# The opening of a one-layer decoder kernel rebuilt: smaller first groups, part of a vector-matrix product on TensorE, half the partial sums returned to PSUM

## The chip, the cores and the metric

The kernel runs on one core of one Trainium2 chip. The metric is the time of one execution on the device, in microseconds (us). The core has a matrix engine (TensorE, PE in the profile; its weight loads are PEld), a vector engine (VectorE, DVE), an activation engine (ScalarE, ACT), GpSimd (POOL) and SyncE (SP), which here only issues DMAs. Each engine runs its own list of instructions in order; the lists wait for each other through semaphores. TensorE adds its results up in PSUM, 8 banks of 128 x 512 f32.

## The reference, cut to what matters

One layer, 256 tokens, model width 2048, everything in float32. A conditioning vector c gives six modulation vectors; two of them (shift1, scale1) shape the normalised input h, and every projection of the layer reads h.

```python
mod = silu(c) @ w_ada + b_ada                  # (2048) @ (2048, 6*2048)
shift1, scale1, gate1, shift2, scale2, gate2 = split(mod, 6)
h = rms_norm(x, norm1_gain) * (1 + scale1) + shift1
proj = h @ w_in                                # (256, 2048) @ (2048, 13840)
# stick-breaking attention, dilated attention, gated linear attention on parts of proj,
# three sigmoid branch gates, an output projection
x = x + gate1 * mixing(h)
h = rms_norm(x, norm2_gain) * (1 + scale2) + shift2
x = x + gate2 * ((silu(h @ w_gate) * (h @ w_up)) @ w_ffn_out)
```

## The kernel before

**Products in three matmuls.** Each weight tile arrives by DMA as f32 (raw), ScalarE casts it to fp32r (whi, line 144), VectorE subtracts to get the remainder (wlo, line 145), and each product is three matmuls (lines 150 to 152): h-high by whi, h-high by wlo, h-low by whi. `load_weights` issues the DMAs on SP's queue, 512 KB (two chunks of 128 rows by 512 columns) at a time, with four buffers each of raw, whi and wlo. `block` runs such a product over a range of 128-row chunks k and both 128-token tiles t, into two PSUM banks.

**The opening.** h needs shift1 and scale1, that is 16.8 MB of w_ada, before its first product. So the 16 chunks of h are made in four groups, `GROUPS = ((0, 3), (3, 7), (7, 11), (11, 16))`. For a group, `ada_group` loads w_ada's columns for these chunks, row chunk by row chunk. VectorE multiplies each piece by the matching column of silu(c) and adds it to an accumulator `ada` (`ada_mac`, lines 245 and 247). At the end one-column matmuls against a column of ones (`column_sum`, line 290) sum the accumulator over its partitions, `finish_columns` (lines 296 and 299) adds the bias and folds in the gain, and `make_h` (lines 370 to 372) writes h's high and low parts for one chunk. A group of five is done in two pieces. While the 13 column blocks A[0..12] of the projection (512 columns each) run over the chunks of group g, `ada_group` for group g+1 is fed in between them, at lower urgency than the weights.

**Partial sums.** The first group's results are copied from PSUM to A[b] by ScalarE (line 400); each later group's are added to A[b] by VectorE (line 402). `orders` turns the order of the blocks round from group to group, and the last block of a group stays in its PSUM banks and is continued by the next group (`carry`). The accumulators of the blocks have four PSUM banks (`psa`), everything else four more (`psm`). In the last group the blocks are mixed with the attention parts, and further projections (r and the gates) that read all of h follow.

**The start.** c comes first, then silu(c). `XAT = 4` pieces of the first group's w_ada are issued ahead of x; then `norm1` squares x on ScalarE (line 349), gets 1/rms (`rsqrt`), scales x on ScalarE (line 356), turns it with 32 PE transposes (line 360) and copies it to xT (line 361). `load_vectors` brings gains and biases: three DMAs on SP's queue, seven on GpSimd's, into scratch tiles shared with norm1, then two transposes.

**Who sets the order.** The program is written as a data flow; a scheduler at build time orders each engine's list by priorities. `prio` raises one, `tc.issue_after` keeps instructions of one engine behind a given one, and `tc.keep_in_program_order` pins one.

Of the kernel before, what the change touches and what calls it, by code (L numbers as in the profile page):

```python
# [10 lines left out]
F32 = mybir.dt.float32  # L11
# [23 lines left out]
XAT = 4  # L35
AHEAD = 4000
FIN = 13
GROUPS = ((0, 3), (3, 7), (7, 11), (11, 16))
# [27 lines left out]
def trunk(ctx: ExitStack, tc: tile.TileContext, I, out):  # L66
# [55 lines left out]
    def load_weights(src, k0, k1, c0, w=NB, spare=()):  # L122
# [6 lines left out]
        with prio():  # L129
# [19 lines left out]
    def mm3(ps, lh, ll, rh, rl, start, stop):  # L149
        nc.tensor.matmul(ps, lh, rh, start=start, stop=False)  # L150
        nc.tensor.matmul(ps, lh, rl, start=False, stop=False)  # L151
        state["mm"] = nc.tensor.matmul(ps, ll, rh, start=False, stop=stop)  # L152

    def block(pss, act, src, k0, k1, c0, base=0, w=None, tiles=range(NT), go_on=False, more=False):
# [3 lines left out]
        for k in range(k0, k1):  # L158
# [6 lines left out]
            for t in tiles:  # L165
                h, l = act(base + k, t)
                mm3(pss[t], h, l, wh, wl, k == k0 and not go_on, k == k1 - 1 and not more)
# [11 lines left out]
    nc.scalar.copy(ones_r, ones)  # L179
# [7 lines left out]
    crow = scr([P, P])  # L187
# [11 lines left out]
    rows = scr([P, P])  # L199
    brow = scr([P, P])  # L200
# [3 lines left out]
    def load_vectors():  # L204
        nc.sync.dma_start(rows[16:32, :], by_chunk("norm1_gain"))
        nc.sync.dma_start(brow[0:96, :], by_chunk("b_ada"))
        nc.sync.dma_start(rows[32:48, :], by_chunk("norm2_gain"))
        for r, name in (
            (ROW_SBQ, "sb_q_gain"),
            (ROW_SBK, "sb_k_gain"),  # L210
            (ROW_DILQ, "dil_q_gain"),
            (ROW_DILK, "dil_k_gain"),
        ):
            nc.gpsimd.dma_start(rows[r : r + 1, :], I[name])
        nc.gpsimd.dma_start(rows[ROW_GB : ROW_GB + 4, :], by_chunk("b_gla_a"))
        nc.gpsimd.dma_start(rows[ROW_GG : ROW_GG + 2, :], by_chunk("gla_out_gain"))
        nc.gpsimd.dma_start(rows[0:16, :], by_chunk("c"))
# [116 lines left out]
    def norm1():  # L334
        xin = [S(f"A{9 + j}", [P, 2, NB]) for j in range(4)]
        for t in range(NT):
            for hf in range(2):
# [3 lines left out]
                )  # L341
        for t in range(NT):
            ss2 = small([P, 2])
            for hf in range(2):
                junk = scr([P, 512])
                xs = xin[2 * t + hf]
                pa = small([P, 2])
                for q in range(2):
                    nc.scalar.activation(junk, xs[:, q, :], AF.Square, accum_out=pa[:, q : q + 1])
                nc.vector.tensor_add(ss2[:, hf : hf + 1], pa[:, 0:1], pa[:, 1:2])  # L350
            ss = small([P, 1])
            nc.vector.tensor_add(ss, ss2[:, 0:1], ss2[:, 1:2])
            rstd = rsqrt(ss, 1.0 / D, [P, 1])
            for hf in range(2):
                xs = xin[2 * t + hf]
                nc.scalar.activation(xs, xs, AF.Copy, scale=rstd)
                for q in range(2):
                    ps = misc_bank([P, 4, P])
                    for i in range(4):
                        nc.tensor.transpose(ps[:, i, :], xs[:, q, i * P : (i + 1) * P], ident)  # L360
                    nc.scalar.copy(xT[2 * hf + q][:, :, t * P : (t + 1) * P], ps)
# [20 lines left out]
    up, down = list(range(13)), list(range(12, -1, -1))  # L382
    orders = (up[1:] + up[:1], up, down)
    carried = []

    def proj_block(g, b, w=None, carry=False):
        k0, k1 = GROUPS[g]
        go_on = bool(carried)
        pss = carried.pop() if go_on else [acc_bank() for _ in range(NT)]
        block(pss, h_at, w_in, k0, k1, b * NB, w=w, go_on=go_on, more=carry)  # L390
# [667 lines left out]
```

## Time and profile before

| | |
|---|---|
| median of 3 runs | 1647.3 us (1646.39 to 1650.2) |
| profiled execution, its own time | 1653.2 us |
| span of the profile (first to last instruction) | 1651.4 us |
| PE, DVE, ACT busy in the span | 1605.1, 1136.2, 773.0 us |
| first projection matmul | 36.88 us |
| mean granted TensorE clock | 0.993 |

The profile is one execution; its span and the 1.8 us around it make its own time. Busy times of different engines overlap and don't add up to the span. A matmul's row ends when its result is out of the pipeline, so matmuls that follow each other overlap in the records; the distance from start to start is what counts. "Granted clock" is the share of full TensorE speed.

### The profile page before, as it was taken

Reading aid. Unit: us, or ns where it says so; the run is one execution under the profiler, and the core shown is the slowest. Engines: PE = TensorE matmul, PEld = TensorE weight load, DVE = VectorE, ACT = ScalarE, POOL = GpSimd, SP = SyncE. Lnnn points to the kernel's source line nnn. Section 1 sums busy time; section 2 is a strip of 40 time slices with the busy share of each in tenths; the row PEclk is TensorE's granted clock in tenths of the full one; section 3 lists DMA queues with packets and bytes.
Section 4 is the critical chain, followed back from the end, with each engine's and each line's share of the span. In section 5 each row is a group of like instructions: output and inputs, shape, how many; then the busy total and the mean of one; then the engine's idle time right before and its main releaser. Section 6 shows DMA issues by size and latency. Waiting matters only on the chain.

```text
span 1651.4 us, 19878 instructions
## 1 busy us (share of the span) xinstructions
PE 1605.1 (97%) x7293; PEld 1324.2 (80%) x7293; DVE 1136.2 (69%) x1367; ACT 773.0 (47%) x1073; POOL 6.0 (0%) x14
## 2 busy tenths in 40 slices
PE   3999999999999999899998999999999999999998
PEld 3788888888878887688887788888888888888887
DVE  5789997787888476866987556766755555554453
ACT  5554446556755444344444644444444444433332
POOL 1000000000000000000000000000000000000000
PEclk8999999999999999999999999999999999999999
DMA  8899986445698778987997467877666566565663
GB/s 299 311 320 323 330 286 217 140 140 166 219 314 296 230 230 309 310 276 263 324 313 268 151 229 258 269 255 258 234 191 190 181 190 192 190 202 194 206 207 111
DMA packets 194561, 395.91 MB, mean 240 GB/s; under 512 B 12898, under 2 KB 27912, under 8 KB 194464
## 3 DMA queue, kind: packets, MB, share of 16 engines
q1 hardware_dynamic: 194240, 394.63, 71.9%
q8 instruction: 57, 0.93, 0.2%
q14 instruction: 40, 0.33, 0.1%
q0 software_dynamic: 224, 0.01, 0.0%
HBM read 392.50 MB, written 2.10 MB: 239 GB/s over the span
## 4 chain that ended last, share of the span: by engine, by line
PE 82%; DMA 7%; DVE 6%; issue 2%; ACT 2%; SPq 1%; DVEq 0%; ACTq 0%
PE acc L150 26%; PE acc L151 26%; PE acc L152 26%; DVE wlo L145 2%; DVE T L247 2%; DMA raw<-w_in 2%; DMA raw<-w_out 2%; ACT whi L144 1%; PE misc L592 1%; PE misc L290 1%; PE misc L846 1%; DVE ada L247 1%; DMA A<-x 1%; DMA raw<-w_br_gla 0%; DMA OS<-w_ada 0%
## 5 line engine op out<-in xcount | busy, mean ns | idle before, releaser
L145 DVE TENSOR_TENSOR wlo<-raw,whi 128x1024 fp32r<-128x1024 f32 (+1 forms) x548 | 653.3, 1197 | 422.2 <-ACT whi L144 420.1
L144 ACT CAST whi<-raw 128x1024 fp32r<-128x1024 f32 (+1 forms) x548 | 563.8, 1032 | 734.2 <-PE acc L152 555.4
L151 PE MATMUL acc<-wlo,H 128*128 128x512 f32 x1576 | 617.7, 392 | 1.7 <-DVE wlo L145 1.7
L150 PE MATMUL acc<-whi,H 128*128 128x512 f32 x1576 | 616.4, 392 | 2.5 <-ACT whi L144 2.5
L152 PE MATMUL acc<-whi,H 128*128 128x512 f32 x1576 | 616.8, 392 | 0.0
L151 PEld LDWEIGHTS acc<-wlo,H 128*128 128x128 f32 x1576 | 297.0, 189 | 64.3 <-DVE wlo L145 4.0
L150 PEld LDWEIGHTS acc<-whi,H 128*128 128x128 f32 x1576 | 296.8, 188 | 64.4 <-ACT whi L144 3.4
L152 PEld LDWEIGHTS acc<-whi,H 128*128 128x128 f32 x1576 | 296.8, 188 | 62.7 <-DVE H L372 0.9
L150 PE MATMUL acc<-whi,A 128*128 128x512 f32 x312 | 123.1, 396 | 2.7 <-ACT whi L144 2.7
L151 PE MATMUL acc<-wlo,A 128*128 128x512 f32 x312 | 123.1, 395 | 1.7 <-DVE wlo L145 1.7
L152 PE MATMUL acc<-whi,A 128*128 128x512 f32 x280 | 110.2, 394 | 0.0
L150 PEld LDWEIGHTS acc<-whi,A 128*128 128x128 f32 x312 | 59.1, 190 | 15.5 <-ACT whi L144 3.5
L151 PEld LDWEIGHTS acc<-wlo,A 128*128 128x128 f32 x312 | 59.5, 191 | 15.0 <-DVE wlo L145 2.9
L152 PEld LDWEIGHTS acc<-whi,A 128*128 128x128 f32 x280 | 53.4, 191 | 11.2
L402 DVE TENSOR_TENSOR A<-A,acc 128x512 f32<-128x512 f32 x72 | 47.9, 684 | 10.2 <-PE acc L152 10.0
L150 PE MATMUL acc<-whi,T 128*128 128x512 f32 x120 | 46.7, 389 | 0.0
L151 PE MATMUL acc<-wlo,T 128*128 128x512 f32 x120 | 46.7, 389 | 0.0
L152 PE MATMUL acc<-whi,T 128*128 128x512 f32 x120 | 46.7, 389 | 0.0
L247 DVE SCALAR_TENSOR_TENSOR ada<-AR,csil,ada 128x1024 f32<-128x1024 f32 x35 | 44.2, 1278 | 0.8 <-DMA AR<-w_ada 0.8
L152 PE MATMUL acc<-whi,OS 128*128 128x512 f32 x112 | 43.6, 389 | 0.0
L247 DVE SCALAR_TENSOR_TENSOR T<-AR,csil,T 128x1024 f32<-128x1024 f32 x30 | 38.1, 1277 | 0.0
L247 DVE SCALAR_TENSOR_TENSOR ada<-OS,csil,ada 128x1024 f32<-128x1024 f32 (+2 forms) x33 | 35.5, 1074 | 1.4 <-DMA OS<-w_ada 1.2
(323 smaller groups left out, 1198.5 us busy)
## 6 DMA issues: line engine op xcount, KB each, us to landing
raw<-w_in SPq DMA_DIRECT2D x205, 512.0 KB, 4.8
raw<-w_ffn_in SPq DMA_DIRECT2D x176, 512.0 KB, 3.7
raw<-w_ffn_out SPq DMA_DIRECT2D x88, 512.0 KB, 4.7
AR<-w_ada SPq DMA_DIRECT2D x69, 512.0 KB, 4.7
KC<-w_ada SPq DMA_DIRECT2D x35, 512.0 KB, 5.9
raw<-w_out SPq DMA_DIRECT2D x32, 512.0 KB, 7.0
KD<-w_ada SPq DMA_DIRECT2D x24, 512.0 KB, 5.6
OS<-w_ada SPq DMA_DIRECT2D x16, 512.0 KB, 6.3
```

The source lines that it names most:

```text
L144: nc.scalar.copy(hi[:, :n, :], raw[:, :n, :])
L145: state["split"] = nc.vector.tensor_tensor(lo[:, :n, :], raw[:, :n, :], hi[:, :n, :].bitcast(F32), op=ALU.subtract)
L150: nc.tensor.matmul(ps, lh, rh, start=start, stop=False)
L151: nc.tensor.matmul(ps, lh, rl, start=False, stop=False)
L152: state["mm"] = nc.tensor.matmul(ps, ll, rh, start=False, stop=stop)
L247: nc.vector.scalar_tensor_tensor(acc, raw, c, acc, op0=ALU.mult, op1=ALU.add)
L290: nc.tensor.matmul(ps, acc, ones[:, 0:1], start=True, stop=True)
L402: nc.vector.tensor_add(A[b][:, t, :], A[b][:, t, :], pss[t])
L592: nc.tensor.matmul(ps[:, h, :], at(lhs, h, t), at(rhs, h, t), start=True, stop=True)
L846: nc.tensor.transpose(ps[:, i, :], src[:, i * P : (i + 1) * P], ident)
```

## The change

The opening is rebuilt; everything from the last group's attention on stays, but for one accumulator of `gla()` that moves from the `psa` banks to the `psm` banks.

- Six groups, of 2, 2, 2, 3, 3 and 4 chunks.
- x is loaded first, then the first group's w_ada (16 pieces of 256 KB), then one w_in piece, all on SP's queue. The vectors go by ScalarE's queue into tiles of their own.
- `norm1` squares x in four instructions and writes 1/rms into two diagonal matrices. `turn_x(j)` then scales and turns a quarter of x in one step, as matmuls of x by the diagonal. The first quarter is turned at the start, the others behind the first three blocks of the first group.
- `first_group` replaces `ada_group` for the first two chunks: VectorE multiplies and adds `ON_PE = 10` of the 16 row chunks; the other six go to TensorE directly, as one-column matmuls with silu(c), into the bank in which the accumulator is summed too (rows 10 to 14, then the accumulator, then row 15).
- The last two blocks of a group stay in PSUM instead of one. Blocks with an odd number that already have a sum get it copied back into PSUM by ScalarE before their matmuls ("seeded"), which then add to it, and ScalarE copies the result out. Even ones are added by VectorE as before.

```diff
-GROUPS = ((0, 3), (3, 7), (7, 11), (11, 16))
+ON_PE = 10
+GROUPS = ((0, 2), (2, 4), (4, 6), (6, 9), (9, 12), (12, 16))
...
     def load_vectors():
-        nc.sync.dma_start(rows[16:32, :], by_chunk("norm1_gain"))
...
-        nc.gpsimd.dma_start(rows[0:16, :], by_chunk("c"))
+        nc.scalar.dma_start(rows[16:32, :], by_chunk("norm1_gain"))
...
+        nc.scalar.dma_start(rows[0:16, :], by_chunk("c"))
...
+    def norm1():
+        part = small([P, 2, NT])
         for t in range(NT):
             for hf in range(2):
+                junk = S(f"H{t}", [P, 2, NB])
+                nc.scalar.activation(junk, xin[2 * t + hf], AF.Square, accum_out=part[:, hf, t : t + 1])
+        ss = small([P, NT])
+        nc.vector.tensor_add(ss, part[:, 0, :], part[:, 1, :])
+        rstd = rsqrt(ss, 1.0 / D, [P, NT])
+        for t in range(NT):
+            nc.scalar.activation(diag[:, t, :], ident, AF.Copy, scale=rstd[:, t : t + 1])
+
+    def turn_x(j):
+        for t in range(NT):
+            ps = misc_bank([P, 4, P])
+            for i in range(4):
+                xs = xin[2 * t + j // 2][:, j % 2, i * P : (i + 1) * P]
+                nc.tensor.matmul(ps[:, i, :], xs, diag[:, t, :], start=True, stop=True)
+            nc.scalar.copy(xT[j][:, :, t * P : (t + 1) * P], ps)
...
-    up, down = list(range(13)), list(range(12, -1, -1))
-    orders = (up[1:] + up[:1], up, down)
+    up = [1, 0] + list(range(2, 13))
+    down = [11, 12] + list(range(10, -1, -1))
+    orders = (down, up, down, up, down[:-2] + [0, 1])
...
     def proj_block(g, b, w=None, carry=False):
         k0, k1 = GROUPS[g]
-        go_on = bool(carried)
-        pss = carried.pop() if go_on else [acc_bank() for _ in range(NT)]
-        block(pss, h_at, w_in, k0, k1, b * NB, w=w, go_on=go_on, more=carry)
+        go_on = bool(carried) and not carry
+        pss, seeded = carried.pop(0) if go_on else ([acc_bank() for _ in range(NT)], False)
+        if not go_on and A[b] is not None and b % 2 == 1:
+            with prio():
+                for t in range(NT):
+                    nc.scalar.copy(pss[t], A[b][:, t, :])
+            go_on = seeded = True
+        block(pss, h_at, w_in, k0, k1, b * NB, w=w, go_on=go_on, more=carry, seeded=seeded)
...
-                if first:
+                if first or seeded:
                     nc.scalar.copy(A[b][:, t, :], pss[t])
                 else:
                     nc.vector.tensor_add(A[b][:, t, :], A[b][:, t, :], pss[t])
...
+    def first_group():
+        w = 2 * P
+        raws = []
+        for i in range(KC // 2):
+            raw = S(f"A{4 + i}", [P, 2, 2, w])
+            for q in range(2):
+                k = 2 * i + q
+                nc.sync.dma_start(
+                    raw[:, q], w_ada[k * P : (k + 1) * P, : 2 * D].rearrange("p (s c) -> p s c", s=2)[:, :, :w]
+                )
+                raws.append(raw[:, q])
+        early.extend(load_weights(w_in, *GROUPS[0], orders[0][0] * NB, ahead=False))
+        norm1()
+        load_vectors()
+        turn_x(0)
+        acc = S("ada", [P, 2, w])
+        for k in range(ON_PE):
...
+        ps = misc_bank([P, 4])
+        nc.tensor.matmul(ps, ident, zero4, start=True, stop=False, skip_group_check=True)
+        cols = [(s, q) for q in range(2) for s in range(2)]
+        for k in range(ON_PE, KC + 1):
+            for i, (s, q) in enumerate(cols):
...
+                nc.tensor.matmul(ps[:, i : i + 1], lhs, rhs, start=False, stop=k == KC, skip_group_check=True)
...
+            if g == 0 and 1 <= n <= 3:
+                with tc.issue_after(state["mm"].ins):
+                    turn_x(n)
+            proj_block(g, b, early if (g, n) == (0, 0) else None, carry=n >= 11)
...
     def gla():
         aw = load_weights(w_in, 0, KC, COL_A, P)
-        ps = acc_bank([P, T])
+        ps = misc_bank([P, T])
```

99 lines of the change are left out of this document (45 added, 54 removed).

## The prediction

> **What bounds the kernel now.** I read the page first, then the busy time by stretches, the chain of waits over the first 100 us, the timeline of the start, and the groups by shape.
>
> ```profile
> span 1651.4 us, 19878 instructions
> PE 1605.1 (97%) x7293; PEld 1324.2 (80%) x7293; DVE 1136.2 (69%) x1367; ACT 773.0 (47%) x1073; POOL 6.0 (0%) x14
> ```
>
> TensorE (PE) is busy in all but 46.3 us of the span. The stretches (length, busy time of PE, PEld, DVE, ACT, POOL, granted clock, DMA share, GB/s) say where those lie:
>
> ```profile
> 0.00:36.88 36.88, 10.75 (x48) 9.66 (x48) 19.96 (x48) 18.40 (x40) 4.27 (x13) 0.95 0.89 306
> 36.88:56.00 19.12, 19.08 (x70) 14.85 (x71) 15.02 (x17) 10.96 (x18) 0.00 (x0) 0.84 0.80 268
> 56.00:59.20 3.20, 1.73 (x7) 0.79 (x6) 1.62 (x2) 3.18 (x5) 0.00 (x0) 1.00 0.86 321
> 60.00:90.00 30.00, 30.00 (x134) 24.85 (x133) 24.34 (x24) 18.32 (x28) 0.00 (x0) 1.00 0.99 350
> 90.00:98.00 8.00, 7.62 (x35) 6.10 (x35) 5.24 (x18) 5.39 (x10) 0.00 (x0) 0.79 0.77 260
> 160.00:240.00 80.00, 80.00 (x363) 66.22 (x363) 76.73 (x111) 36.05 (x41) 0.00 (x0) 1.00 0.91 303
> ```
>
> The first projection matmul starts at 36.88 us, and PE idles 26.1 us before it. From 36.88 to 240 the stops are small: 1.47 us at 56 to 59.2, 0.38 us at 90 to 98. The clock costs more. A mean of 0.84 over 19.12 us is 6.1 us at half speed, so 3.1 us lost; 0.79 over 8 us loses 1.7 us. In the third group (160 to 240) PE is full while DVE is busy 76.73 of 80 us. So two things can move the time: where the stream starts, and whether DVE and DMA, both nearly full, keep feeding it. The chain of waits (start, us, what) and the timeline show what holds the start:
>
> ```profile
> 21.76 6.85 DMA OS<-w_ada
> 33.03 1.85 PE misc L290 x8
> 35.29 0.60 ACT H L370
> 35.89 0.94 ACT whi L144
> 92.72 1.24 DVE wlo L145
> 94.56 0.43 PE acc L152
> 97.91 0.23 PE acc L152
> 159.60 1.77 PE misc L290 x16
> 349.50 1.78 PE misc L592 x16
> ```
>
> ```profile
> 14.78 0.16 DVE L350 TENSOR_TENSOR tiny<-tiny 128x1 f32<-128x1 f32 x1 [0.27 <-ACT scr L349]
> 16.59 2.19 ACT L356 ACTIVATE A<-A,tiny 128x1024 f32<-128x1024 f32 x2 [0.19 <-DVE tiny L236]
> 17.80 3.67 PE L360 MATMUL misc<-ident,A 128*128 128x128 f32 x16 [15.06 <-ACT A L356]
> 18.10 0.52 POOL L217 DMA_DIRECT2D scr<-c  x1
> 33.03 2.69 PE L290 MATMUL misc<-ones,ada 128*128 128x1 f32 x12 [3.14 <-DVE ada L247]
> ```
>
> The chain is w_ada's bytes, DVE's last products, column sums, two columns of modulation, one chunk of h, one cast, stream. The DMA answer for the first 40 us (one number a microsecond) gives the bytes:
>
> ```profile
> GB/s 0 8 97 356 379 309 274 279 239 379 424 410 400 398 392 376 370 358 138 69 67 86 350 370 330 301 329 349 351 378 401 400 401 389 383 387 383 272 41 199
> A<-w_ada SPq DMA_DIRECT2D x10, 384.0 KB, 8.4
> A<-x SPq DMA_DIRECT2D x4, 512.0 KB, 10.7
> raw<-w_in SPq DMA_DIRECT2D x3, 512.0 KB, 9.2
> scr<-c POOLq DMA_DIRECT2D x1, 8.0 KB, 3.7
> ```
>
> From 2 to 18 us the mean is 340 GB/s. Then come four slices near 90 GB/s: the vectors, which wait for a scratch tile, hold up w_ada behind them on SP's queue.
>
> **The start, worked out.** Three chunks' w_ada (16 x 384 KB) become two (16 x 256 KB, 0.262 MB each); x (2.10 MB) goes first, one w_in piece (0.524 MB) last; the vectors leave SP's and GpSimd's queues. With no hole in the queue, at 340 GB/s from 2 us: x is in at 8.2, the eleventh w_ada piece (the first that PE takes) at 2 + (2.10 + 11 x 0.262)/0.340 = 16.7, the last at 20.5, w_in at 22.0.
>
> x's side: the last square ends about 1.1 us (half of L356's 2.19) after landing, at 9.4; a sum and rsqrt took 1.8 us (14.78 to 16.59), so 11.2; two copies into diag of 128 columns each (estimated at 0.35, under the 0.42 of L372's 256 below), 11.9; the first quarter's 8 matmuls. An fp32 matmul is two instructions in the records (L592: 8 matmuls, x16), so 16 x 0.229 (L360's 3.67/16) = 3.7, to 15.6: ahead of the w_ada pieces. DVE's ten products at 0.75 (row below) end at 18.7.
>
> PE's part: 28 column sums, 56 instructions. L290 took 2.69/12 = 0.224 us each at the start but 1.77/16 = 0.111 at 159.60, the clock being the difference. From 16.7 that is 12.5 us (end 29.2) or 6.2 us (end 22.9). [...] The last sum (34.88) to the end of h (35.89) took 1.0 us, so the stream starts at 25.7, the cast having been made under it. **Saved: 36.9 - 25.7 = 11.2 us** (6.7 to 13.0).
>
> [...]
>
> **The stream after it.** Three quarters of x are turned inside the first group: 24 matmuls, 48 instructions at 0.111 (L592) = **+5.3**, and +0.5 because the first of them meet a slow clock. Before, x's 32 transposes lay in PE's idle time. Column sums: 52 instructions after the start become 56, **+0.4**. The 1.47 at 56, the 0.38 and 1.7 at 90 to 98 belong to group ends and a w_in queue that are rebuilt: **-3.6** if nothing takes their place.
>
> What may take it: DVE, ACT and DMA per group. The rows (by shape):
>
> ```profile
> L145 DVE TENSOR_TENSOR wlo<-raw,whi 128x1024 fp32r<-128x1024 f32 x81 | 97.7, 1220 | 14.7 <-ACT whi L144 14.4
> L144 ACT CAST whi<-raw 128x1024 fp32r<-128x1024 f32 x81 | 85.0, 1052 | 83.5 <-PE acc L152 45.6 <-DVE A L402 17.7 <-DMA raw<-w_in 16.1
> L402 DVE TENSOR_TENSOR A<-A,acc 128x512 f32<-128x512 f32 x56 | 37.1, 683 | 5.5 <-PE acc L152 5.4
> L247 DVE SCALAR_TENSOR_TENSOR ada<-OS,csil,ada 128x1024 f32<-128x1024 f32 x16 | 20.5, 1279 | 0.1
> L400 ACT COPY A<-acc 128x512 f32<-128x512 f32 x26 | 15.3, 589 | 23.6 <-PE acc L152 22.6
> L247 DVE SCALAR_TENSOR_TENSOR ada<-OS,csil,ada 128x768 f32<-128x768 f32 x9 | 9.0, 1000 | 1.2 <-DMA OS<-w_ada 1.2
> L247 DVE SCALAR_TENSOR_TENSOR ada<-OS,csil,ada 128x512 f32<-128x512 f32 x8 | 6.0, 748 | 0.1
> L372 DVE TENSOR_TENSOR H<-scr,H 128x256 fp32r<-128x256 f32 x16 | 6.5, 419 | 0.7 <-ACT scr L371 0.6
> ```
>
> A group of two chunks is 13 x 12 matmuls at 0.23 = 35.9 us of PE. In the new third group DVE has 13 x 1.21 for wlo, 16 x 1.00 for the next three chunks' products, 6 blocks' sums (12 x 0.66) and 3 x 0.42: 40.9 us, 5.0 over. Counted in the same way (26 x 1.21, 16 x 1.75, 26 x 0.66, 5 x 0.42), the old third group has 78.7 against 71.8, 6.9 over, and PE did not stop there: rows overlap a little, and four buffers of split weights carry a lead. The other groups are even or under. DMA needs 16 x 0.393 + 13 x 0.524 = 13.1 MB there, 37.4 us at 60 to 90's 350 GB/s, 1.5 over, with four raw buffers of lead. ACT gets 50 copies into PSUM and 50 out more, 59 us by L400; it is busy 36 of 80 us in the old third group, so has room, but in a two-chunk block of 2.8 us two copies out and two in (2.4) must fit before the block after next. A cast in between (1.05) makes it 3.4, 0.6 over; with ten such blocks, 0 to 6. I take 0, since the second bank is wanted only three matmuls (0.7) later. A lighter DVE (72 sums become 60, -7.9 us) gains nothing by itself where PE is full. Blocks 11 and 12 of each group now stay in PSUM over the change of group, twice the cover of before, but there are five changes, not three. New stops in all: 0 to 15.5 (five changes at 90 to 98's 2.1 and the whole 5.0); I take **+3.5**, nearer to the rows of 160 to 240. The last group shrinks from five chunks to four, 13 x 6 x 0.23 = 17.9 us less cover under attention; the same matmuls run earlier, and the other projections stand ready behind: 0.
>
> **Sum**: -11.2 + 5.3 + 0.5 + 0.4 - 3.6 + 3.5 = -5.1 us. The profiled execution took 1653.2 (span 1651.4 and 1.8 around it), 5.9 above the median of 1647.3. So about 1648.1 in a profile, and a median of **1642.2**.
>
> **Rivals.**
> *Fast sums* (0.2): the clock rises during the first turn of x and holds. Sums end at 22.9, the stream starts 1.8 earlier and without its 3.1 of slow clock: -10.0, 1637.3. For it: PE would have been at work without a break since 11.9. Against: the 90 us row above. [...] With no new stops either it is -13.5, 1633.8.
> *Slow sums, or late vectors* (0.12), where "shared with TensorE" does not do what it says: 56 x 0.224 puts the stream at 30.2, 4.5 later: -0.6, 1646.7. Ten DMA issues on ACT's queue (about 0.5 each by L217, landing 3.7 later) between the norm and the first copies, with PE's transposes of them ahead of the sums, would cost the same 5 us.
> *Short groups starve* (0.2), the other sign: DVE enters the third group without a lead. Its in-order queue then meets the column sums with wlo behind them, as at 92.72 (L145, then 0.43 a matmul instead of 0.23). All five changes cost 2.1 and the third group its 5.0: 15.5 for my 3.5 gives +6.9, 1654.2. It turns the sign beyond 0.2% from 12 us of new stops on. For it: DVE over by 5.0 and short blocks. Against: 160 to 240 ran as full with PE at 80.00.
>
> **How the numbers follow.** The forecast's case has 0.48, with a range of its own from 1637 to 1648. A measurement here can tell some 0.2%, 3.3 us, from no change. Faster: 0.36 of the 0.48, all of fast sums, 0.02 of slow sums: 0.58. Same: 0.07 + 0.08 + 0.02 = 0.17. Slower: 0.05, 0.02 and 0.18 of the short groups: 0.25. The range, 1634 to 1654, takes in fast and slow sums whole and leaves out the upper half of the short groups and small tails.
>
> **What would show it.** First acc matmul at 24 to 27 us (30 says slow sums); L290's successors at 0.11 or 0.22 each; 48 turn instructions in the first 40 us of the stream; the DMA row without the hole at 18 to 22; PE idle between 70 and 250 under 5 us in total; PEclk below 1.0 only at the start. Wrong: a start after 31, or PE idle over 12 us in the groups, with DVE at the end of the waits.

## The result, and the profile after

The changed kernel is slower. Its median is 1662.6 us (1658.1 to 1667.0, five runs) against 1648.1 us (1646.4 to 1650.2, five runs); the ratio is 1.0084, 95% interval 1.0061 to 1.0106. The forecast was 1642.2 us, range 1634 to 1654. The profiled execution of the changed kernel took 1661.2 us (span 1659.4), that of the kernel before 1653.2 us, itself some 5 above its median. So the two traces show 8.0 of the 14.5 us between the medians.

I cut the span in two. The **start** goes to the first projection matmul. The **stream** goes from there to the issue of the first `w_br_sb` piece, where the branch projections begin. Behind that point the kernels have the same code. The two ends (start us, us; the second row is the timeline's answer for the tile: issues, duration, first and last start), of before and of after:

```profile
36.88 1.22 PE L150 MATMUL acc<-whi,H 128*128 128x512 f32 x2 [1.16 <-ACT whi L144]
L133 SPq DMA_DIRECT2D raw<-w_br_sb x12: 367/368/796, 558.6 to 777.5; - x12
```

```profile
34.28 1.22 PE L150 MATMUL acc<-whi,H 128*128 128x512 f32 x2 [3.62 <-ACT whi L144]
L133 SPq DMA_DIRECT2D raw<-w_br_sb x12: 368/368/617, 567.0 to 784.7; - x12
```

The start was to become 11.2 us shorter and became 2.6 shorter. The stream went from 521.7 to 532.7, 11.0 longer where 6.1 was forecast. Behind it both traces take the same: 1651.4 - 558.6 = 1092.8 and 1659.4 - 567.0 = 1092.4. That stretch is not steady, though: over the traces of all sixteen kernels below it took from 1086.1 (before_no_hole) to 1092.8 us, with the same code. A single trace's span can be off by several us for that alone.

The page of after, then the stream of before and of after, then stretches of after (columns as in the prediction's windows):

```profile
PE 1617.9 (97%) x7375; PEld 1334.3 (80%) x7375; DVE 1125.9 (68%) x1357; ACT 824.5 (50%) x1166; POOL 1.8 (0%) x7
```

```profile
36.88:558.60 521.72, 517.92 (x2430) 426.28 (x2431) 440.82 (x649) 293.19 (x516) 1.75 (x1) 0.99 0.76 253
34.28:567.00 532.72, 525.19 (x2482) 430.83 (x2483) 438.55 (x653) 351.47 (x625) 1.09 (x1) 0.99 0.77 250
```

```profile
0.00:34.28 34.28, 15.03 (x78) 14.46 (x78) 11.65 (x34) 11.30 (x24) 0.70 (x6) 0.82 0.89 293
34.28:56.00 21.72, 21.62 (x109) 18.16 (x110) 15.65 (x18) 14.86 (x22) 0.00 (x0) 0.89 0.83 264
180.00:190.00 10.00, 8.91 (x44) 7.32 (x43) 8.67 (x19) 5.73 (x9) 0.00 (x0) 0.96 0.89 293
190.00:200.00 10.00, 10.00 (x40) 8.07 (x39) 7.16 (x12) 7.28 (x13) 0.00 (x0) 0.87 0.82 282
250.00:260.00 10.00, 8.73 (x48) 7.21 (x47) 7.41 (x20) 5.31 (x9) 0.00 (x0) 1.00 0.92 324
```

TensorE is busy 12.8 us longer than in before: 4.3 ahead of the first projection matmul, 7.3 in the stream and 1.2 behind. In the stream it also idles longer, 7.5 us (532.72 - 525.19) for 3.8 (521.72 - 517.92). New idle places are 1.09 us at 180 to 190 and 1.27 at 250 to 260. After the first of them the granted clock is 0.87 in the mean over ten us. The timeline of the start (start us, us, engine, line, operation; in brackets the idle time and its releaser) tells why the stream starts late:

```profile
1.19 5.82 SPq L343 DMA_DIRECT2D A<-x  x4
6.89 1.28 ACT L181 ACT_TABLE_LOAD   x1 [6.89 <-DMA H<-dil_q_gain]
8.27 1.05 ACT L353 ACTIVATE H<-A 128x1024 f32<-128x1024 f32 x1
15.53 3.49 PE L366 MATMUL misc<-H,A 128*128 128x128 f32 x16 [4.39 <-ACT H L359]
20.17 7.08 PE L464 MATMUL misc<-csil,A 128*128 128x1 f32 x40 [1.04 <-DMA A<-w_ada]
27.11 1.85 PE L464 MATMUL misc<-ones,ada 128*128 128x1 f32 x8
28.82 1.84 PE L464 MATMUL misc<-csil,A 128*128 128x1 f32 x8
31.21 0.60 ACT L376 ACTIVATE H<-T,mod 128x256 fp32r<-128x256 f32 x1 [11.58 <-DVE mod L302]
33.19 2.93 ACT L144 CAST whi<-raw 128x1024 fp32r<-128x1024 f32 x3
```

Four delays stand in a row. ScalarE issues ten vector DMAs first and loads its table only at 6.89, so the first square starts at 8.27. The first piece that TensorE takes lets it start at 20.17, not 16.7. The 56 column sums take to 30.66. And the cast of the first `w_in` piece comes behind the four instructions of h, at 33.19. The DMA answer for the first 40 us, and the longest wait of SP's queue for x (us in total, times, longest):

```profile
GB/s 0 15 99 201 340 395 80 217 281 379 283 264 369 378 368 346 350 350 347 347 349 348 357 377 364 357 378 371 379 365 376 367 246 6 0 0 47 299 359 315
SPq L343 <- DMA A<-x: 3.9, 1, 3.9
```

The hole at 18 to 22 us is gone as meant. In its place x's last piece waits 3.9 us on SP's queue, the slices from 6 to 12 us are thin, and at 33 to 36 us nothing moves: all four buffers of `w_in` are full and wait for the late cast and its split.

In the stream, the chain of waits (start, us, what) shows x's quarters and the handovers between groups. The last row is what TensorE waited for there (us in total, times, longest):

```profile
39.74 1.78 PE misc L366 x16
44.28 1.78 PE misc L366 x16
48.80 1.78 PE misc L366 x16
65.12 1.02 PE misc L293 x8
179.53 6.64 DMA OS<-w_ada
187.33 1.50 PE misc L293 x12
247.74 4.39 DMA OS<-w_ada
253.55 1.95 PE misc L293 x16
PE misc L293 <- DVE ada L250: 2.4, 2, 1.3
```

The quarters are 3 x 1.78 = 5.3 us. At the last two of the five handovers (the sums at 187.33 and 253.55) the last piece of `w_ada` lands late; VectorE's last product and the column sums wait for it, 2.4 us in all. (For shift1 and scale1 the opening loads 2 x 16.8 = 33.6 MB of `w_ada` in all; the text on the kernel before gives 16.8, which is one of the two.)

### The profile page after: what moved, and what is told of

It is laid out like the page before. It is cut to its first block, busy times and chain, and to the rows that moved or that the text cites. A ratio compares the mean times of both kernels' runs of the same rounds, so it can differ in the third digit from the quotient of the medians.

```text
span 1659.4 us, 20136 instructions
## 1 busy us (share of the span) xinstructions
PE 1617.9 (97%) x7375; PEld 1334.3 (80%) x7375; DVE 1125.9 (68%) x1357; ACT 824.5 (50%) x1166; POOL 1.8 (0%) x7
## 4 chain that ended last, share of the span: by engine, by line
PE 80%; DMA 9%; DVE 5%; ACT 3%; issue 2%; SPq 0%; DVEq 0%; ACTq 0%
PE acc L151 25%; PE acc L152 25%; PE acc L150 25%; DMA raw<-w_out 2%; DMA raw<-w_in 2%; DVE wlo L145 2%; DVE T L250 2%; ACT whi L144 1%; PE misc L644 1%; DMA raw<-w_br_gla 1%; PE misc L293 1%; DMA A<-w_ada 1%; PE misc L898 1%; DMA OS<-w_ada 1%; DMA AR<-w_ada 1%
## 5 line engine op out<-in xcount | busy, mean ns | idle before, releaser
L417 ACT COPY A<-acc 128x512 f32<-128x512 f32 x76 | 43.3, 586 | 22.9 <-PE acc L152 21.1
L419 DVE TENSOR_TENSOR A<-A,acc 128x512 f32<-128x512 f32 x60 | 38.9, 682 | 5.8 <-PE acc L152 5.8
L250 DVE SCALAR_TENSOR_TENSOR ada<-OS,csil,ada 128x512 f32<-128x512 f32 (+2 forms) x40 | 38.5, 962 | 2.4 <-DMA OS<-w_ada 2.1
```

Of the source, the lines that this page charges most:

```text
L250: nc.vector.scalar_tensor_tensor(acc, raw, c, acc, op0=ALU.mult, op1=ALU.add)
L417: nc.scalar.copy(A[b][:, t, :], pss[t])
L419: nc.vector.tensor_add(A[b][:, t, :], A[b][:, t, :], pss[t])
```

## The experiments

The theory after the comparison: the start is late because the one-column sums run at the slow clock behind late pieces, and the stream is longer by x's quarters and by `w_ada`'s pieces landing late at handovers. The rivals: the sums returned to PSUM, the place of the cast, the ten vector DMAs, or the number of groups is the cause.

Start and stream are read in each trace as above; the times are medians, the ratios are to the kernel before, run beside them. The row of after has its own runs of before (1648.1); the next four kernels share another set (1648.2), then four (1646.5), three (1650.2) and three (1648.3). Kernels of different sets are best compared by their ratios.

| kernel | start us | stream us | time us | ratio, 95% interval |
|---|---|---|---|---|
| before | 36.9 | 521.7 | 1648.1 | |
| after | 34.3 | 532.7 | 1662.6 | 1.0084, 1.0061 to 1.0106 |
| after_again | 34.5 | 534.3 | 1663.9 | 1.0091, 1.0077 to 1.0105 |
| no_return | 37.6 | 537.7 | 1667.1 | 1.0109, 1.0093 to 1.0126 |
| pool_queue | 32.8 | 540.5 | 1664.2 | 1.0091, 1.0077 to 1.0105 |
| three_sets_on_pe | 32.0 | 528.4 | 1654.4 | 1.0038, 1.0026 to 1.0051 |
| early_pieces | 30.9 | 532.8 | 1656.4 | 1.0059, 1.0046 to 1.0072 |
| old_groups | 41.9 | 526.6 | 1659.0 | 1.0078, 1.0066 to 1.0091 |
| pool_after_ident | 29.9 | 530.1 | 1654.6 | 1.0046, 1.0033 to 1.0058 |
| before_no_hole | 34.4 | 520.8 | 1646.4 | 1.0004, 0.9992 to 1.0016 |
| turns_first | 30.9 | 524.3 | 1644.2 | 0.9954, 0.9940 to 0.9968 |
| cast_first | 35.2 | 537.2 | 1664.6 | 1.0084, 1.0069 to 1.0098 |
| four_short_first | 28.1 | 534.0 | 1655.9 | 1.0034, 1.0021 to 1.0048 |
| turns_first_ten | 33.8 | 525.3 | 1653.2 | 1.0032, 1.0017 to 1.0047 |
| turns_and_pool | 29.2 | 524.9 | 1642.6 | 0.9961, 0.9945 to 0.9977 |
| warm_only | 33.7 | 535.1 | 1662.9 | 1.0094, 1.0065 to 1.0122 |

**The changed kernel once more**, unedited, as the mark for the others.

> The changed kernel once more, as the base of this call. Theory 'start': the stream begins at 34.3 us and not at 25.7, because x waits behind the vectors, the one-column sums run slowly, and the cast comes after h; the 5.3 us of x's turns are then not paid for. Theory 'groups': the short groups stop TensorE at the handovers. Both expect 1.006 to 1.011 of the kernel before, a first projection matmul at 34 to 35 us, and a w_ada piece that is late at one or two handovers (1 to 1.5 us each).

It repeated: start 0.2 later, stream 1.6 longer, the time within the interval. The code of the start is the same in no_return, the next kernel, and its trace begins the stream at 37.6. So start and stream, each read from one trace, carry differences of 3 us and of 1.6 us that come from the run and not from the kernel.

**No sums back into PSUM**

```diff
-        if not go_on and A[b] is not None and b % 2 == 1:
+        if False:
```

> The changed kernel without the return of sums to PSUM: all later sums are added by VectorE (110 instead of 60 additions, 33 us more for VectorE, 100 copies less for ScalarE). If VectorE bounds the short groups (theory 'groups'), this is slower than the changed kernel by 10 us or more, with waits on wlo and on the products. If the start is what is wrong (theory 'start'), it still costs, but under 5 us. If the copies into PSUM are what stops TensorE (rival), it is faster by 3 us or more.

Slower by 3.2 us than after_again (the intervals overlap a little), with a stream 3.4 longer, and a start, which the edit does not touch, 3.1 later. TensorE waits for VectorE instead, at the start of groups:

```profile
PE acc L152 <- DVE H L378: 5.1, 2, 4.0
PE acc L151 <- DVE wlo L145: 2.2, 5, 0.6
```

Returning half the sums takes work off VectorE where the short groups need it; without it the kernel is no faster, so it is not what made the change slow.

**The vectors by GpSimd's queue**

```diff
-        nc.scalar.dma_start(rows[16:32, :], by_chunk("norm1_gain"))
+        nc.gpsimd.dma_start(rows[16:32, :], by_chunk("norm1_gain"))
...
```

> The changed kernel with the vectors' ten DMAs on GpSimd's queue, still in tiles of their own. Theory 'start': x's third and fourth piece no longer wait 4 us for the vectors, and ScalarE's first activation starts at 3 us instead of 8; x's squares end 3 to 4 us earlier, w_ada lands 3 us earlier, and the stream begins 3 to 4 us earlier, at 30 to 31 us. Theory 'groups': the stream begins earlier but the total moves by under 1 us, since the handovers wait for w_ada all the same.

The start came 1.5 us earlier than in after, the stream was 7.8 longer, the time as in after. ScalarE's table load came at 0.73 and x's four issues took 1.92 us, but the identity was made behind the DMAs on GpSimd here, and the first square still waited until 8.86. The sums' row is the useful part: they follow the turning with no pause, and are slow all the same.

```profile
15.66 3.79 PE L366 MATMUL misc<-H,A 128*128 128x128 f32 x16 [2.03 <-ACT H L359]
19.53 8.67 PE L464 MATMUL misc<-csil,A 128*128 128x1 f32 x40
28.06 1.84 PE L464 MATMUL misc<-ones,ada 128*128 128x1 f32 x8
```

All at 0.22 to 0.23 us an instruction, for 12 us without a break, twice the 0.111 of other places. Those 12 us of one-column sums did not bring the rate up. (The granted clock reads 1.00 over this whole stretch, from 15.66 to 31.6, so a slow clock is the author's reading of the rate here. In after, where the granted clock falls from 1.00 to 0.50 at 22.0 us, the sums go from 0.11 to 0.22 us each with it.)

**Fewer sums on TensorE: three sets of sums, not seven**

```diff
-ON_PE = 10
+ON_PE = 14
```

> The changed kernel with ON_PE = 14: VectorE takes 14 of the 16 pieces, TensorE only two and the accumulator, 12 sums (24 instructions) for 28 (56). If the sums are bound by TensorE's rate (0.18 to 0.22 us an instruction in the profile after), the sums end 4 to 6 us earlier and the stream begins at 29 to 30 us. If they are bound by the landing of w_ada, it moves by under 1 us. Theory 'groups': the total moves by under 2 us either way.

24 sum instructions in place of 56. Start 32.0, stream 528.4, and 9.5 us off the time. In this kernel the first cast is also done ahead of h, at 27.19, and the seven-set version's wait for it is gone. So fewer sums helped, but in the traces the gain has more in the stream (5.9) than at the start (2.5). Why fewer sums shorten the stream was not tried by itself. The next kernels build on this one.

**w_ada's pieces asked for earlier in each group**

```diff
-FIN = 13
+FIN = 11
```

(with ON_PE = 14)

> ON_PE = 14 as in three_sets_on_pe (1654.4 us), and FIN = 11 for 13: the next group's w_ada pieces are asked for over 11 blocks of a group and not 13. If the stops at the handovers come from a last piece asked for too late (theory 'groups'), the two waits of the column sums (1 to 3 us each) go: 2 to 5 us faster than three_sets_on_pe. If the short groups are bound by VectorE's total work (rival), the stops only move and the time stays within 1.5 us.

No gain: 1.0059 against 1.0038, the stream 4.4 longer. Asking for the pieces earlier does not cure the late ones.

**The old four groups in the changed kernel**

```diff
-GROUPS = ((0, 2), (2, 4), (4, 6), (6, 9), (9, 12), (12, 16))
+GROUPS = ((0, 3), (3, 7), (7, 11), (11, 16))
```

(with ON_PE = 14; the first group's tiles and sums widened to three chunks, one tile for each piece)

> ON_PE = 14 as in three_sets_on_pe, but with the old four groups (0-3, 3-7, 7-11, 11-16): the first group has three chunks, so 6.3 MB of w_ada before the stream and 18 sums for 12. Theory 'start': w_ada's last bytes land 6 us later and the sums take 2.7 us more, so the stream begins at 40 to 41 us for 32; nothing comes back later, and the time is 6 to 9 us over three_sets_on_pe. Theory 'groups': from the first matmul to the first weight of the branch projections it takes 523 to 526 us for 528 in three_sets_on_pe, since three handovers replace five; the time is then 3 to 6 us over three_sets_on_pe.

The stream is 526.6, 4.9 over the kernel before, and the chain has x's quarters in it and no late piece:

```profile
48.16 1.78 PE misc L366 x16
54.04 1.78 PE misc L366 x16
59.92 1.78 PE misc L366 x16
```

So under the old groups the stream is longer by about the quarters' 5.3 us. The 1.8 us more of three_sets_on_pe, with short groups, is no more than two traces of one kernel differ by. But a first group of three chunks starts at 41.9, ten later than one of two. The short first group pays: 1654.4 against 1659.0, 1.0038 against 1.0078.

**The vectors by GpSimd's queue, behind the identity**

```diff
-    make_identity(nc, ident)
+    with tc.high_priority(offset=60000):
+        make_identity(nc, ident)
```

(and the `nc.gpsimd` lines of pool_queue, with ON_PE = 14)

> ON_PE = 14, and the vectors on GpSimd's queue with the identity made ahead of all but one of them (in pool_queue it came behind them, at 8.5 us, and c's transpose with it). Theory 'start': ScalarE's squares begin at 5 us for 8.3, w_ada lands 2 to 3 us earlier, the stream begins at 28 to 30 us for 32.0; 2 to 4 us faster than three_sets_on_pe. Theory 'groups': the stream begins earlier, and the gain is lost again at the handovers, as pool_queue lost its 1.5 us; the time stays within 1.5 us of three_sets_on_pe.

The start came 2.1 us before that of three_sets_on_pe, the stream was 1.7 longer, and the time was the same; both differences are of the size that single traces carry.

**The kernel before without its hole**: its vectors moved to GpSimd's queue and to tiles of their own, the identity first, nothing else.

```diff
-    rows = scr([P, P])
-    brow = scr([P, P])
+    rows = S("H6", [P, P])
+    brow = S("H5", [P, P])
...
-        nc.sync.dma_start(rows[16:32, :], by_chunk("norm1_gain"))
+        nc.gpsimd.dma_start(rows[16:32, :], by_chunk("norm1_gain"))
```

> The kernel before with one change: the vectors go by GpSimd's queue into tiles of their own, so nothing on SP's queue waits for the norm's scratch tiles. Its DMA rate falls to about 90 GB/s from 18 to 22 us; without that the last w_ada lands about 3 us earlier. Theory 'start': the first projection matmul moves from 36.9 to about 34 us and the time falls by about 3 us (0.998 of before). If what the start gains is lost again later (theory 'groups', or a DMA bound), it stays within 1 us of before.

The hole went and the start came 2.5 us earlier; the time did not move by more than the measurement's width (1.0004, 0.9992 to 1.0016). Whether those 2.5 us were kept is not settled.

**All of x turned ahead of the sums**

```diff
-        turn_x(0)
+        for j in range(4):
+            turn_x(j)
         acc = S("ada", [P, 2, w])
...
-            if g == 0 and 1 <= n <= 3:
-                with tc.issue_after(state["mm"].ins):
-                    turn_x(n)
```

(with ON_PE = 14)

> three_sets_on_pe with all four quarters of x turned one after the other ahead of the sums, none within the stream. In three_sets_on_pe the first projection matmul came at 32.0, the stream took 528.4 us, and the first quarter was turned by 20.6 with TensorE then idle to 25.1. Theory (the three quarters cost the stream 5.3 us of TensorE and nothing else): the stream falls to 523. What the start then costs depends on the clock. If matmuls of 128 columns bring the clock up, the second quarter takes 3.5 us and the third and fourth 1.8 each, to 27.7, the 24 one-column sums then take 0.11 us each, and the stream begins at 31 to 32: time 1649, ratio 1.001. Rival (the clock stays at 0.22 a matmul until the long matmuls run): quarters to 31.1, sums 5.6 more, stream begins at 38, and the time stays at 1654 to 1655. Second rival (the copies of the turned quarters on ScalarE cost the stream, not the turns): the stream stays at 528.

The best so far: 1644.2 us, 0.9954 (0.9940 to 0.9968), faster than the kernel before, and 10 us below three_sets_on_pe (14 by the ratios). Its start:

```profile
15.43 10.19 PE L366 MATMUL misc<-H,A 128*128 128x128 f32 x64 [4.37 <-ACT H L359]
25.60 1.03 PE L465 MATMUL misc<-csil,A 128*128 128x1 f32 x8
27.39 1.19 PE L465 MATMUL misc<-csil,A 128*128 128x1 f32 x8
30.85 0.80 PE L150 MATMUL acc<-whi,H 128*128 128x512 f32 x1 [2.28 <-ACT H L376]
```

64 instructions in 10.19 us are 0.159 each, under the first quarter's 0.22: the rate rose on the way. (In warm_only, below, the first 16 take 3.78 us and the 48 behind them 5.59.) The eight sums of a piece then take 1.03 us, not 1.85. So 48 instructions more on TensorE ahead of the stream left its start no later (30.9 against 32.0), and the stream became 4.1 shorter. The spans of the two traces differ by 6.6; the profiled run of turns_first (1647.5) was its slowest, so part of the 10 us is in no trace.

**The first cast ahead of h**

```diff
-        with prio():
+        with prio(), tc.issue_after(state["cast"].ins):
             h_group(0)
```

(`state["cast"]` is the latest cast of `load_weights`; ON_PE stays at 10)

> The changed kernel as it is (ten pieces on VectorE, vectors by ScalarE's queue), but the four instructions of h are ordered behind the cast of the first w_in piece, which was done behind them at 33.2 to 34.2. Theory (the cast's place alone cost the start 2.4 us, the sums' slow clock the rest): first projection matmul at 31.8 to 32.0 in place of 34.3 to 34.5, sums as long as before (7 us for the 40 and 1.85 for each eight), stream 532.7 to 534.3 as before; time 1661 against 1663, ratio 1.0075. That would leave three_sets_on_pe's gain of 9.5 us to the stream, not to the start. Rival (a stream that starts earlier meets the same last pieces of w_ada at the second handover and waits for them): start gains 2.4, stream longer by 2.4, time as before.

The forecast of the start missed. The cast no longer holds the stream: from the last sum to the first projection matmul it is 1.2 us in place of 3.6. But the 40 sums took 8.69 us from 21.92 in this trace, in place of 7.08 from 20.17, and the start was 35.2. In no_return, without this edit, they were as late and as slow (8.70 from 21.90). The time is that of after, with an interval 2.4 us to either side. So the cast's place was in the trace's last wait, and the 2.4 us it was to bring do not show in the time.

**Four groups with a short first one**, on top of turns_first and pool_after_ident

```diff
-GROUPS = ((0, 2), (2, 4), (4, 6), (6, 9), (9, 12), (12, 16))
+GROUPS = ((0, 2), (2, 5), (5, 10), (10, 16))
```

> The parts that helped put together: three pieces' sums on TensorE, vectors by GpSimd's queue behind the identity, all of x turned ahead of the stream, and four groups of 2, 3, 5 and 6 chunks, so three handovers and not five. Against pool_after_ident (start 29.9, stream 530.1): the quarters take 5.3 out of the stream, two handovers fewer take out 1.4 of sums and what was waited at them. Theory (the stream's floor is the 521 of the kernel before): start at 30 to 31 if turning warms the clock, stream 521 to 523, end of the stream at 552 to 553 against 558.6 in the kernel before: time 1641, ratio 0.9965. Rival (the first group of two chunks asks for three chunks of w_ada and two of w_in, 13.1 MB in 34 us or 385 GB/s, over the 360 to 395 that the start reached at best): TensorE waits 3 to 5 us at the first handover, stream 525 to 527, time 1645, ratio 0.999.

The earliest start of all, 28.1, and a stream of 534.0: 1655.9 us. Neither theory had it. TensorE did not wait at the handovers but within the groups, for split weights:

```profile
PE acc L151 <- DVE wlo L145: 9.5, 12, 1.2
```

Here two chunks must cover the products of three, and three those of five. VectorE is busy 46.9 of the 53 us from 65 to 118, and from 65 to 210 ScalarE's casts wait 38.4 us for pieces of `w_in` to land; which of the two holds the splits was not separated. Six groups that grow slowly do not show this wait (0.5 us in turns_first).

**The turning ahead of all 56 sums**

```diff
-        turn_x(0)
+        for j in range(4):
+            turn_x(j)
```

(turns_first's edits and cast_first's, with ON_PE = 10)

> The changed kernel with its ten pieces on VectorE and 56 sums, all of x turned ahead of the sums, and the four instructions of h ordered behind the first cast. Theory (moving the turning brings the clock up before the sums and takes 5.3 us from the stream): turning 15.5 to 25.6 as in turns_first, 40 sums at 0.125 in 5.0, the rest to 33, start at 34 to 35 and no earlier than in the changed kernel; stream 524 to 527 in place of 532.7 to 534.3; time about 1652, ratio 1.001 to 1.003: between turns_first (0.9954) and the changed kernel (1.0084), the three us of start and the rest of the stream. Rival (the sums were slow by their own kind): 40 sums in 8.7, start at 39, time 1657. Second rival (turns_first gained from having fewer sums): time above 1660.

Start 33.8, stream 525.3, 1653.2 us. With it, four kernels cross two choices (medians, ratios to before):

| | x turned in the stream | x turned ahead of the sums |
|---|---|---|
| 56 sums on TensorE | after_again: 1663.9, 1.0091 | turns_first_ten: 1653.2, 1.0032 |
| 24 sums on TensorE | three_sets_on_pe: 1654.4, 1.0038 | turns_first: 1644.2, 0.9954 |

Each choice is worth about 10 us whatever the other is: turning ahead 10.7 and 10.2 us, fewer sums 9.5 and 9.0 (9 to 14 us by the ratios). In the traces, start and stream together show 9.7 and 5.2 of the first, 8.4 and 3.9 of the second. So giving TensorE six row chunks in place of two (which also takes four products off VectorE) costs about as much as turning x in the stream, and the two together are more than the whole loss of the changed kernel. (The kernels other than after_again also cast the first piece ahead of h, for which cast_first shows no gain in the time.)

**turns_first with the vectors by GpSimd's queue**

```diff
-        nc.scalar.dma_start(rows[16:32, :], by_chunk("norm1_gain"))
+        nc.gpsimd.dma_start(rows[16:32, :], by_chunk("norm1_gain"))
...
```

> turns_first with the vectors issued by GpSimd's queue behind the identity. In four_short_first, whose start is the same, the first projection matmul came at 28.1; turns_first had it at 30.9 and a stream of 524.3. Theory (an earlier start is kept): start 28.1, stream 524 to 525, time 1641.5 against 1644.2 for turns_first, ratio 0.9940. Rival (the stream is held to when the last pieces of w_ada of each group land, so an earlier start waits longer at the handovers, as pool_after_ident gave back 1.7 of 2.1): stream 526 to 527, time 1644, ratio 0.9955.

1642.6 us, 0.9961 (0.9945 to 0.9977). Faster than the kernel before; from turns_first the measurement can't tell it. The start came at 29.2, not 28.1, and the trace's stream was 0.6 us longer than that of turns_first.

**Only warmth**: cast_first with 24 matmuls that nobody reads between the first quarter and the sums.

```diff
         turn_x(0)
+        for n in range(6):
+            idle = misc_bank([P, 4, P])
+            for i in range(4):
+                nc.tensor.matmul(idle[:, i, :], xin[n % 4][:, 0, i * P : (i + 1) * P], diag[:, n % 2, :], start=True, stop=True)
```

> cast_first with 24 useless matmuls of 128 columns between the first quarter of x and the sums; their results are read by nobody. In cast_first the 40 sums took 8.69 us from 21.9, the last eight ended at 34.0, and the stream began at 35.2. Theory (the clock is down, and matmuls bring it up): the 24 end at 24.5 to 26, the 40 sums take 4.6 to 5.0, the last end at 31, start at 32 to 32.5: 3 us earlier for more work. Rival (one-column sums take 0.22 us each whatever ran ahead of them): sums end at 38, start at 39. What the time makes of 3 us at the start: 1661 if the stream keeps them, 1664 if the handovers take them back.

```profile
19.23 5.59 PE L448 MATMUL misc<-H,A 128*128 128x128 f32 x48
24.80 4.61 PE L468 MATMUL misc<-csil,A 128*128 128x1 f32 x40
29.27 1.54 PE L468 MATMUL misc<-ones,ada 128*128 128x1 f32 x8
30.67 1.85 PE L468 MATMUL misc<-csil,A 128*128 128x1 f32 x8
33.72 1.22 PE L150 MATMUL acc<-whi,H 128*128 128x512 f32 x2 [1.21 <-ACT H L376]
```

5.6 us of useless work made the 40 sums 4.1 us shorter than in cast_first (4.61 for 8.69), 0.115 us an instruction in place of 0.22. So what ran ahead of the sums set their rate, and not their kind. For the clock, which the theory names: the granted clock is 0.98 in the mean from 20 to 30 us, and 0.51 from 30 to 40, where the last eight take 0.23 each. In cast_first it reads 1.00 in both stretches, with the 40 sums at 0.22, so there the slow clock is read from the rate alone. With nothing but sums behind the wide matmuls the rate fell again. As a way to an earlier start it was worth little: the stream began 1.5 us before that of cast_first, and 1.3 of that is a turning that began earlier in this trace (15.66 for 16.98). The time, 1662.9 us, does not show 1.5 us (interval 1.0065 to 1.0122).

This kernel and turns_first_ten have the same start (33.7 and 33.8) and the same amount of TensorE work ahead of it. They differ in whether that work turns x or is thrown away, and x is then turned in the stream. The times differ by 9.6 us, the streams by 9.8 (the spans by 4.9, since the stretch behind the stream was short in the trace of warm_only). The quarters are 5.3 us of the 9.8. For the rest, TensorE's waits for the sums at handovers (to 560 us), VectorE's waits for `w_ada` (to 260), and two stretches around the last two handovers, of warm_only first:

```profile
PE misc L293 <- DVE ada L250: 4.2, 2, 2.2
DVE ada L250 <- DMA OS<-w_ada: 4.3, 4, 1.2
186.00:200.00 14.00, 12.09 (x53) 9.74 (x52) 8.84 (x19) 6.36 (x11) 0.00 (x0) 0.88 0.81 272
250.00:270.00 20.00, 17.45 (x78) 13.90 (x77) 15.14 (x30) 10.73 (x18) 0.00 (x0) 0.91 0.81 271
```

```profile
PE misc L293 <- DVE ada L250: 0.9, 2, 0.6
DVE ada L250 <- DMA OS<-w_ada: 1.5, 4, 0.8
186.00:200.00 14.00, 13.37 (x65) 10.99 (x64) 11.75 (x26) 9.75 (x16) 0.00 (x0) 1.00 0.86 295
250.00:270.00 20.00, 19.77 (x96) 16.36 (x95) 15.40 (x30) 15.90 (x37) 0.00 (x0) 1.00 0.87 293
```

With the quarters in the stream `w_ada`'s pieces land later and the handovers wait 3.3 us longer. Behind both stops the granted clock falls (0.88 and 0.91 in the mean), which it does not in turns_first_ten; 0.12 x 14 + 0.09 x 20 is 3.5 us lost. Over the whole stream TensorE is busy 8.5 us longer (the quarters and the slow clock) and idle 1.3 us longer, which makes the 9.8. Why the pieces land later is open. SP's waits for buffers add up to the same in both (153.0 and 151.3 us to 260). ScalarE has each quarter's copy from PSUM between its casts (L367); whether that copy delays the splits was not tried by itself.

## Why the prediction was wrong, step by step

**How the error adds up.** In the traces the forecast was -5.1 us and +8.0 was measured. Of these 13.1 us the start holds 8.6 and the stream 4.9 (11.0 for 6.1); the rest of the span gives 0.4 back. The median missed by 20.4. The other 7.3 us are in how single traces lie to their medians: before's 5.1 above, after's 1.4 below, and a median of before that became 0.8 higher with two more runs.

**The start (11.2 saved; 2.6 measured)** failed in four terms.

*The first piece for TensorE*: forecast at 16.7, sums began at 20.17, 3.5 late. The sum let 340 GB/s flow from 2 us on; the row shows 201 and less until 4 us, and 80 to 283 in five of the six slices from 6 to 12. I had put "the vectors leave SP's queue" at nothing on the start, and priced ten issues on ScalarE's queue only in a rival, as delaying copies behind the norm. They came ahead of it: table load at 6.89, the first square at 8.27. That is only a part of it. x's side, forecast to be turned by 15.6, was too short by itself: in pool_after_ident, with the vectors on GpSimd's queue and the identity first, the second square still waits for x until 9.51, it and the two behind it then follow each other on ScalarE to 12.55 where the sum had one square behind the landing, and the turning starts at 14.95, not 11.9.

*The sums*: 24.7 - 16.7 = 8.0 us forecast, 10.5 measured, 2.5 more. The stream's start at 25.7, less the 1.0 us of h, puts the last sum at 24.7, between the 22.9 and 29.2 of the two rates: the author's estimate, with slow sums first and fast ones behind, and no run shows that term. TensorE began at 15.53, and in pool_queue 12 us of sums did not bring the rate up. In after the order was the reverse: the granted clock is 1.00 until 21.5 us, behind the turning, and 0.50 from 22 us to the end of the sums, and they go from 0.11 to 0.22 us each. The rival of slow sums had the slow rate, and was given 0.12; its 12.5 us for 56 sums were measured in pool_queue (12.1), not in after.

*The end of h*: "1.0 us" was one chunk's; two chunks are four instructions on ScalarE, 2.6 us from the last sum, 1.6 more.

*The cast* "made under it": it was queued behind h, 1.0 more. 3.5 + 2.5 + 1.6 + 1.0 = 8.6. The run cast_first qualifies the last two: with the cast ahead of h its trace has 1.2 us in place of the 3.6 behind the last sum, but its time does not move by what the measurement can tell.

**The sums on TensorE as a choice.** The prediction counted 56 sum instructions and did not ask what fewer would do. With 24 of them the time is 9.0 and 9.5 us lower, in both kernels that differ in it. In the traces 2.5 and 2.9 us of that are at the start; how the rest arises is open.

**Turning x in the stream (+5.3)**: right in its own instructions (3 x 1.78). The step that failed is that this was all: in time it is worth about 10 us (10.7, 10.2 and, from warm_only to turns_first_ten, 9.6). In the streams it is 9.8 us in that last pair, 4.1 with 24 sums. What comes on top there is longer stops at two handovers and the slow clock behind them. Its slow-clock term (+0.5) was not paid: the first quarter in the stream took 1.78 like the others.

**Column sums (+0.4)**: mis-sized. The chain has 1.02 + 1.02 + 1.36 + 1.50 + 1.95 = 6.85 us of them over five handovers, 5.48 in the kernel before: +1.4.

**Old stops go, new ones come (-3.6 + 3.5)**: net nothing was forecast. The idle time of TensorE in the stream grew by 3.7 us. With the quarters and the sums that makes 10.4 of the stream's 11.0. The size of the new stops was judged well; that the old ones' going would pay for them was not, and the place was not. The forecast had VectorE over its time in the third group, but from 70 to 250 us TensorE idles only 1.1 us, and the stops at 180 to 190 and at 250 to 260 wait for late bytes of `w_ada`. The larger part lies elsewhere: up to 300 us the idle time grew by 1.0 us, behind it by 2.8, at 460 to 540 us, where the last group runs among the attention parts. The prediction had put the last group's 17.9 us less cover at 0. In the twelve traces whose last group has four chunks TensorE idles 2.6 to 5.1 us from 300 us to the end of the stream, in the four with five or six chunks 1.6 to 3.2. The ranges overlap; it fits less cover, but was not tried by itself.

**Half the sums back into PSUM (0)**: not refuted. Taking it out cost 3.2 us in no_return, at overlapping intervals; if it is anything, it is a gain.

**The rivals.** Short groups starve had the right sign and 1654.2, but not by what it said: VectorE did not hold the third group, and the short first group pays for itself by its start (old_groups). No rival combined a late start with a longer stream, and both happened. **The tell-tales**: a start after 31 was named as wrong, and it came; the hole at 18 to 22 went and TensorE idled under 5 us from 70 to 250, as forecast. The clock was not slow only at the start (0.87 at 190 to 200), and "30 says slow sums" missed the 34.3, to which the other terms of the start add.

**What stays open.** The medians differ by 14.5 us and the traces by 8.0. The profiled execution of before took 5 us more than the median of its runs, and where those runs are shorter can't be said from one trace. In before_no_hole, whose code behind the start is that of before, the stream is 0.9 us and the stretch behind it 6.7 us shorter, so the difference may lie there.

## What to carry to other kernels

Ask whether work sits in an engine's idle time or where that engine is the bound. Ahead of the sums, 48 turning instructions did not make TensorE's stream start later (30.9 against 32.0); in the stream, where TensorE is busy 525 of 533 us, they cost their 5.3 us and what they disturbed. Moving x's turning back ahead of the sums was worth about 10 us, and taking four of the six row chunks off TensorE again was worth 9 to 10; together they turn a loss of 0.8% into a gain of 0.5%. When a step's rate depends on the clock, ask what runs just before it and whether the rate holds while the step runs (0.115 us a sum behind 9 us of wide matmuls, 0.23 six us later). An earlier start need not arrive at the end: 1.5 and 2.1 us at the start brought no time in pool_queue and pool_after_ident, whose streams were 7.8 and 1.7 us longer. And one trace for each kernel is not enough to account for a few us: the same start code gave 34.3 to 37.6 here.

## What the runs showed of the hardware

- One-column fp32 matmuls took 0.115 us an instruction behind 9 us of 128-column ones, and 0.22 to 0.23 in pool_queue, where 12 us of nothing else did not change it. In warm_only the rate fell between 4.5 and 5.9 us after the last wide matmul (24.82 to 29.27 and 30.67); in after the granted clock fell at 22.0 us, 3 us behind the turning that ended at 19.02. Behind the same 16 turning instructions the 40 sums took 7.08 us in after, 6.88 in after_again and 8.69 in cast_first.
- Ten small DMAs on ScalarE's queue cost more than the 0.23 to 0.54 us that each took to issue in after: ScalarE's table load waited to 6.89, and x's four issues on SP's queue took 5.82 us, one waiting 3.9. With the same ten DMAs on GpSimd's queue (pool_queue) the table load came at 0.73 and x's issues took 1.92 us.
